# An output projection whose matmuls stand in source order on TensorE, with another pace of attention and eight k tiles left for later

## The chip, the cores and the metric

The kernel runs on one core of a Trainium2 chip. The time is the device time of one execution in microseconds; the figure shown is the median of three executions. The engines are named as in the profile: PE (TensorE, matmuls and transposes), DVE (VectorE), ACT (ScalarE), POOL (GpSimd) and SP (SyncE, which only issues transfers).

## The reference

One block of a hybrid network on a sequence of 512 tokens, width D = 2048, all in float32. In short:

```python
u   = rmsnorm(x)                                  # [512, 2048]
p   = u @ w_in                                    # z, conv input, dt, q, six k/v, gates
ys  = ssd_mixer(z, xbc, dt)                       # state space half, 1024 wide
ya  = nsa_mixer(q, kc, vc, ks, vs, kw, vw, gate)  # attention half, 1024 wide
h   = x + concat(ys, ya) @ w_out                  # output projection, 2048 -> 2048
t   = rmsnorm(h)
out = h + (silu(t @ w_gate) * (t @ w_up)) @ w_down   # FFN, 5632 wide
```

The attention half has 4 groups of 4 heads. Each head attends over compressed blocks, over selected blocks and in a window; with 512 tokens the last two are two full causal attentions, here called branches.

## The kernel before

**Products.** Every operand is split in a rounded part (hi, made by `a_hi` on ACT, L124) and the rest (lo, made by a subtraction on DVE, L127). A product of one 128-deep k tile is three matmuls, hi·hi, hi·lo and lo·hi (L233 to L235), 128x512 each. This is the unit in which work is counted: a *k tile*.

**Units.** `run_unit` computes one block of 128 output columns from its k tiles. 41 units of 16 k tiles make p from w_in. Then come 16 units, c0 to c15, of the output projection: their right side is what the state space half (k tiles 0 to 7) and attention (8 to 15) produced. Since the last heads' outputs aren't ready in time, unit c takes only its first NS[c] k tiles (11, 11, then 12); the remainder is made later by *oa steps* (first matmul at L1175 to L1177), which load the rest of w_out anew, add it to what the unit left in DRAM (h1_d) and prepare the FFN's input. Weights arrive by SP (`wraw`), four k tiles at a time, and are split on ACT (`whi`) and DVE (`wlo`) ahead of use.

**What runs between k tiles.** Attention, the evacuations and the state space half are generators. `Sched.tick()` is called once after each k tile and moves each generator on; what a generator yields is the number of ticks until it goes on. Attention of one group makes 32 scores (head, branch, block of 128 queries), in 36 loop steps. A step does: one score (two matmuls, L833 and L834, then a fused maximum on DVE, L837, and the exponential on ACT, L839); a yield of 1; the transposes of the score three steps earlier (LAG, L862), whose result is split to `pth` on ACT and `ptl` on DVE; the normalisation; and a yield of `PACE[...]`, which is 1. After each fourth score the products with v follow (L872, L873, L878, into ps_v). I call four such steps a round. After a pair of heads the output `at` is split to `u`, the right side of the later units. The 128 scores of all groups are counted through as score steps here.

**The evacuation of an output unit** (`ev_os`, L981 to L992): ACT copies PSUM to a tile h1 (L987); POOL issues a transfer that adds x to it (L988), and after four ticks one that stores it to h1_d (L990). While attention's pool is open h1 is one single buffer. Before c15, `pre_last` waits until attention has been issued to its end, then closes attention's pool and opens those of the oa steps and the FFN (Z, A, R, E), which lie on the same memory, and loads h1 of the first four blocks from ACT's queue (L1220; the fourth goes to `rrow`).

**Order.** What the ticks fix is the source order. Around the change a scheduler of the Tile framework makes each engine's order from it: it follows the source's order as a priority but by its own estimate of times lets an instruction that it takes for ready go ahead of one that it takes for late. Most of the FFN's steps are already under `tc.manual_schedule()`, which keeps the source order. Each engine runs its own list strictly in that order.

Of the kernel before, what the change touches and what calls it, by code (L numbers as in the profile page):

```python
# [24 lines left out]
          (0, 6), (2, 3), (6, 5), (7, 6), (5, 6), (3, 6), (4, 6), (1, 6)]  # L25
GRING = 7

NS = [11, 11] + [12] * 14
KSUB = 4
PACE = [1]  # L30
LAG = 3
EB = 5
LEAD = 3
# [36 lines left out]
NU = 41  # L70
# [44 lines left out]
def body(ctx, tc, xT, w_in, w_out, w_gate, w_up, w_down, w1k, w1v, cols, rows, kst, out):  # L115
# [100 lines left out]
    def run_unit(u):  # L216
        if u.pre:
            u.pre()
        if u.need:
            sch.run_until(*u.need)  # L220
        n_u = st["unit"] = st.get("unit", 0) + 1
        if n_u > 6:
            sch.run_until(("evac", n_u - 2))
        p = ps_t() if n_u <= 2 else ps_s() if n_u <= 4 else ps_g()
        p = p[:, 0:u.cols[1] - u.cols[0]]
        for i, k0, n in u.sub:
            issue_split(i)
            for j in range(n):
                if j == 0:
                    issue_split(i + LEAD)  # L230
                k = k0 + j
                ah, al = [t[:, u.cols[0]:u.cols[1]] for t in u.rhs(k)]
                pe.matmul(p, hi_t[i][:, j, :], ah, start=(k == 0), stop=False)  # L233
                pe.matmul(p, hi_t[i][:, j, :], al, start=False, stop=False)  # L234
                pe.matmul(p, lo_t[i][:, j, :], ah, start=False, stop=(k == u.nk - 1))  # L235
                sch.tick()
            del hi_t[i], lo_t[i]

        def evac():
            yield from u.evac(p)  # L240
            sch.flags.add(("evac", n_u))
        sch.add(evac())
# [339 lines left out]
    P2 = {}  # L582
# [203 lines left out]
    def attention():  # L786
# [6 lines left out]
        for g in range(4):  # L793
# [105 lines left out]
            n = len(items)  # L899
            for s in range(n + LAG + 1):  # L900
                if s < n:
                    score(*items[s])
                    if items[s][1:] == (1, 3):
                        sch.flags.add(("h", g, items[s][0]))
                yield 1
                if 0 <= s - LAG < n:
                    trans(*items[s - LAG])
                if s < n:
                    norm(*items[s])
                yield PACE[s % len(PACE)]  # L910
                if 0 <= s - LAG - 1 < n and items[s - LAG - 1][2] == 3:
                    pvmm(*items[s - LAG - 1][:2])
            sch.flags.add(("a", g))
# [42 lines left out]


    def pre_out():
        sch.run_until(*[("gy", t) for t in range(8)])
        P2["ms"] = [(U[:, 0, k], U[:, 1, k]) for k in range(8)]  # L960
        P2["ma"] = [(U[:, 0, 8 + k], U[:, 1, 8 + k]) for k in range(8)]
        for k in range(8):
            h_, l_ = P2["ms"][k]
            t = wp.tile([128, 512], F32, tag="raw", name="gy", bufs=4)
            nc.sync.dma_start(t, gy_d[k])
            mul(pool, t, t, P2["row2"])
            a_hi(h_, t, scale=col(C_SN + k))
            dve.scalar_tensor_tensor(l_, t, col(C_SN + k), f(h_), op0=ALU.mult, op1=ALU.subtract)  # L968
        sch.add(ma_in(P2["at"] + 1))
# [768 lines left out]
    def run_rest():  # L1738
        pre_steps()
        for s in steps[:KD]:  # L1740
            run_step(s)
        with tc.manual_schedule():
            for s in steps[KD:]:
                run_step(s)
            sch.drain()
        for n in ("ta", "E", "ws"):
            close_pool(n)
        right.close()
# [52 lines left out]
    for n, u in enumerate(units):  # L1801
        if n == 4:
            nc.sync.dma_start(kcs(K_AM, NK - K_AM), kst[:, K_AM:NK])
            nc.sync.dma_start(colc[:, C_PE:C_W2], cols[:, C_PE:C_W2])
        run_unit(u)
    run_rest()


# [86 lines left out]
```

## Time and profile before

| | |
|---|---|
| median of three executions | 2248.61 us (2246.32 to 2249.75) |
| the profiled execution | 2251.17 us, span 2249.4 us |
| mean granted clock of PE | 0.988 |
| PE busy | 2164.1 us, 96% of the span |
| DVE / ACT / POOL busy | 1785.6 / 1192.9 / 430.5 us |
| c0 begins, attention ends, first matmul of the oa steps | about 600, 821 and 828 us |

How to read it: a row of windows gives, for a stretch of the span, each engine's busy time with its count of instructions, then the clock that PE was granted (1.00 is full), the busy share of the DMA engines and what they moved. A row of a timeline gives start, duration, engine, line, operation and tiles, and in brackets how long the engine stood idle before it and what ended that. An engine with a q behind its name is its queue, issuing transfers.

### The profile page before, as it was taken

How to read it: one execution, taken by the hardware profiler on the slowest of the kernel's cores; microseconds unless marked ns; L12 is line 12 of the kernel's file. 1: busy time of each engine (PE TensorE's matmuls, PEld its weight loads, DVE VectorE, ACT ScalarE, POOL GpSimd, SP SyncE). 2: the span in 40 equal slices, each digit the busy share in tenths (PEclk: the TensorE clock that was granted, in tenths of full speed). 3: DMA queues.
4: the chain of work that ended last, by engine and by line, in shares of the span. 5: the costliest groups of instructions: out<-in, count | busy, mean ns of one | idle time of the engine just before them, and what ended most of it. 6: DMA issues, size and time to landing. Idle time of an engine off the chain costs nothing. (4 is left out here: it accounts for less than half of the span.)

```text
span 2249.4 us, 35036 instructions
## 1 busy us (share of the span) xinstructions
PE 2164.1 (96%) x12892; PEld 1903.7 (85%) x12892; DVE 1785.6 (79%) x2822; ACT 1192.9 (53%) x1992; POOL 430.5 (19%) x440
## 2 busy tenths in 40 slices
PE   7999999999999988999999999999999899999996
PEld 5888888888877866788888888888888899999996
DVE  7799766678776648888888788888888888988897
ACT  4564456567665646555555555555555443433353
POOL 2011224133241116100000000001000121222222
PEclk9999999999999989999999999999999999999999
DMA  5222343222244447787888878888887969696985
GB/s 178 90 71 76 120 151 101 74 82 74 94 119 121 109 132 213 203 244 210 246 229 241 227 221 240 219 252 229 222 242 221 338 224 318 187 303 167 297 192 143
DMA packets 170860, 417.18 MB, mean 185 GB/s; under 512 B 16848, under 2 KB 24032, under 8 KB 170688
## 3 DMA queue, kind: packets, MB, share of 16 engines
q1 hardware_dynamic: 99200, 246.99, 33.2%
q0 software_dynamic: 28192, 80.91, 18.5%
q10 hardware_dynamic: 43296, 87.04, 10.7%
q8 instruction: 101, 1.65, 0.3%
q14 instruction: 71, 0.58, 0.1%
HBM read 353.80 MB, written 57.41 MB: 183 GB/s over the span
## 5 line engine op out<-in xcount | busy, mean ns | idle before, releaser
L124 ACT ACTIVATE R<-Z 128x1024 fp32r<-128x1024 f32 (+4 forms) x461 | 417.2, 918 | 450.2 <-DVE Z L136 308.1
L127 DVE TENSOR_TENSOR R<-Z,R 128x1024 fp32r<-128x1024 f32 (+4 forms) x371 | 388.8, 1057 | 27.7 <-ACT R L124 22.6
L234 PE MATMUL ps_g<-u,whi 128*128 128x512 f32 x782 | 309.2, 395 | 2.1 <-DVE u L968 2.1
L233 PE MATMUL ps_g<-u,whi 128*128 128x512 f32 x782 | 310.2, 398 | 0.0
L235 PE MATMUL ps_g<-u,wlo 128*128 128x512 f32 x782 | 309.4, 396 | 0.0
L1171 PE MATMUL ps_s<-u,R 128*128 128x512 f32 (+1 forms) x1136 | 252.9, 350 | 8.6 <-ACT A L1381 8.4
L127 DVE TENSOR_TENSOR wlo<-wraw,whi 128x512 fp32r<-128x512 f32 x212 | 161.2, 762 | 80.7 <-ACT whi L124 80.1
L1171 PEld LDWEIGHTS ps_s<-u,R 128*128 128x128 f32 x1136 | 184.6, 188 | 40.9 <-ACT A L1381 15.1
L124 ACT ACTIVATE whi<-wraw 128x512 fp32r<-128x512 f32 x212 | 132.5, 625 | 138.3 <-PE ps_g L234 95.8
L234 PEld LDWEIGHTS ps_g<-u,whi 128*128 128x128 f32 x782 | 147.5, 189 | 31.3 <-DVE u L968 3.3
L235 PEld LDWEIGHTS ps_g<-u,wlo 128*128 128x128 f32 x782 | 147.4, 189 | 28.8
L233 PEld LDWEIGHTS ps_g<-u,whi 128*128 128x128 f32 x782 | 147.2, 189 | 27.4
L1171 PE MATMUL ps_t<-u,R 128*128 128x512 f32 (+1 forms) x608 | 131.8, 347 | 0.3 <-DVE R L127 0.3
L1171 PE MATMUL ps_g<-u,R 128*128 128x512 f32 (+1 forms) x608 | 131.8, 347 | 0.3 <-DVE R L127 0.3
L1171 PE MATMUL ps_g<-T,R 128*128 128x512 f32 (+1 forms) x568 | 128.1, 353 | 3.6 <-DVE R L127 3.6
L1171 PE MATMUL ps_s<-V,R 128*128 128x512 f32 (+1 forms) x560 | 124.6, 350 | 5.0 <-ACT V L124 3.3
L1171 PE MATMUL ps_s<-T,R 128*128 128x512 f32 (+1 forms) x584 | 126.3, 347 | 0.7 <-DVE R L127 0.7
L127 DVE TENSOR_TENSOR E<-Z,R 128x1024 fp32r<-128x1024 f32 (+1 forms) x90 | 109.2, 1213 | 3.1 <-ACT R L124 1.8
L1171 PEld LDWEIGHTS ps_t<-u,R 128*128 128x128 f32 x608 | 98.9, 188 | 14.8 <-DVE R L127 0.7
L1171 PEld LDWEIGHTS ps_g<-u,R 128*128 128x128 f32 x608 | 98.9, 188 | 14.8 <-DVE R L127 0.7
L136 DVE TENSOR_TENSOR A<-ps_g,A 128x512 f32<-128x512 f32 (+1 forms) x110 | 71.1, 653 | 48.5 <-PE ps_g L1171 39.1
L1171 PEld LDWEIGHTS ps_g<-T,R 128*128 128x128 f32 x568 | 94.6, 192 | 17.5 <-DVE R L127 4.0
(490 smaller groups left out, 5544.6 us busy)
## 6 DMA issues: line engine op xcount, KB each, us to landing
Z<-in_w_up SPq DMA_DIRECT2D x95, 512.0 KB, 5.2
Z<-in_w_gate SPq DMA_DIRECT2D x94, 512.0 KB, 6.8
wraw<-in_w_in SPq DMA_DIRECT2D x164, 256.0 KB, 2.6
g_d<-A ACTq DMA_DIRECT2D x22, 1792.0 KB, 15.0
Z<-in_w_gate POOLq DMA_DIRECT2D x39, 512.0 KB, 7.0
Z<-in_w_up POOLq DMA_DIRECT2D x38, 512.0 KB, 8.7
Z<-in_w_down SPq DMA_DIRECT2D x56, 320.0 KB, 5.2
Z<-in_w_down SPq DMA_DIRECT2D x40, 384.0 KB, 4.1
```

What stands on the lines that cost most here:

```text
L124: act.activation(dst, src, AF.Copy, scale=scale)
L127: eng.tensor_tensor(dst, src, f(hi), ALU.subtract)
L136: eng.tensor_tensor(o, a, b, ALU.add)
L233: pe.matmul(p, hi_t[i][:, j, :], ah, start=(k == 0), stop=False)
L234: pe.matmul(p, hi_t[i][:, j, :], al, start=False, stop=False)
L235: pe.matmul(p, lo_t[i][:, j, :], ah, start=False, stop=(k == u.nk - 1))
L1171: pe.matmul(o, w, x, start=start, stop=(k == n - 1 and o is q), skip_group_check=not fresh[0])
```

## The change

Four edits. NS of the last unit goes from 12 to 8, so that its oa step makes 8 k tiles instead of 4. PACE goes from 1 to 2, 2, 2, 3 in turn, for as long as w_in's units run; from `pre_out` (ahead of c0) on attention takes PACE_OUT, 1, 2, 1, 2. And all output units are issued under a manual schedule for PE alone: its instructions stand in source order from c0 on, while ACT, DVE, POOL and SP are still ordered by the scheduler.

```diff
-NS = [11, 11] + [12] * 14
+NS = [11, 11] + [12] * 13 + [8]
 KSUB = 4
-PACE = [1]
+PACE = [2,2,2,3]
+PACE_OUT = [1,2,1,2]
...
                 if s < n:
                     norm(*items[s])
-                yield PACE[s % len(PACE)]
+                yield P2.get("pace", PACE)[s % len(PACE)]
...
     def pre_out():
+        P2["pace"] = PACE_OUT
         sch.run_until(*[("gy", t) for t in range(8)])
...
+        if n == NU:
+            break
         run_unit(u)
+    with tc.manual_schedule(engines={mybir.EngineType.PE}):
+        for u in units[NU:]:
+            run_unit(u)
     run_rest()
```

NU is the number of w_in's units. The number of instructions on PE is the same, 12876; the first 1750 rows of its order and the last 3706 stand as before. Score step 72 stands at k tile 656 of the program before and at 658 now. From score step 68 to 84 there are 122 instructions of DVE and 36 k tiles before, and 124 and 28 now. Lines of the changed kernel are one higher than before behind PACE, and two higher behind `pre_out`.

Three places show what moved. The first is PE where c0 and c1 meet. Before (ps_g_6967 is c0, ps_g_7107 is c1), the two blocks' k tiles alternate, and scores and transposes stand between them:

```order
L235 MATMUL ps_g_7107<-u_91,wlo_7032 128x512
L833 MATMUL ps_s_6392<-kh_5379,rq_5857 128x128
L834 MATMUL ps_s_6392<-kl_5380,rq_5857 128x128
L233 MATMUL ps_g_6967<-u_91,whi_6824 128x512
L233 MATMUL ps_g_7107<-u_91,whi_7031 128x512
L872 MATMUL ps_v_6381<-cph_5930,vpad_3170 128x512
```

Now (c1 is ps_g_6738) a run of scores and transposes without any k tile stands behind c0, and c1 begins after it:

```order
L879 MATMUL ps_v_6522<-ptl_6440,v_4947 128x128
L834 MATMUL ps_s_6680<-kh_5097,rq_5293 128x128
L835 MATMUL ps_s_6680<-kl_5098,rq_5293 128x128
L863 MATMUL ps_t_6687<-ident_74,e_6581 128x128 x2
L834 MATMUL ps_s_6694<-kh_5097,rq_5293 128x256
L835 MATMUL ps_s_6694<-kl_5098,rq_5293 128x256
L863 MATMUL ps_t_6701<-ident_74,e_6617 128x128 x3
L834 MATMUL ps_s_6710<-kh_5097,rq_5293 128x384
L835 MATMUL ps_s_6710<-kl_5098,rq_5293 128x384
L863 MATMUL ps_t_6717<-ident_74,e_6646 128x128 x4
L834 MATMUL ps_s_6726<-kh_5097,rq_5293 128x512
L835 MATMUL ps_s_6726<-kl_5098,rq_5293 128x512
L234 MATMUL ps_g_6738<-u_91,whi_6507 128x512
```

The eleven k tiles of c0 no longer share their stretch with those of c1.

The second is ACT behind the evacuation of c3, where the load of c3's h1 (to rrow_75) stands; it waits for c3's store. Before:

```order
L987 ACTIVATE h1_7559<-ps_g_7389 128x512
L124 ACTIVATE e_6636<-e_6636,em_6637 128x128
L124 ACTIVATE e_6657<-e_6657,em_6658 128x256
L124 ACTIVATE whi_7615<-wraw_7455 128x512
L124 ACTIVATE pth_6605<-ps_t_6643 128x2x128
L1220 DMA rrow_75<-h1_d_66 128x512
L124 ACTIVATE pth_6605<-ps_t_6664 128x3x128
L839 ACTIVATE e_6699,em_6700<-e_6699,em_6700 128x384
```

Now:

```order
L989 ACTIVATE h1_7172<-ps_g_7026 128x512
L840 ACTIVATE e_7168,em_7169<-e_7168,em_7169 128x256
L125 ACTIVATE pth_7112<-ps_t_7185 128x3x128
L125 ACTIVATE whi_7219<-wraw_7074 128x512
L840 ACTIVATE e_7202,em_7203<-e_7202,em_7203 128x384
L125 ACTIVATE pth_7112<-ps_t_7209 128x4x128
L125 ACTIVATE pth_7238<-ps_t_7240 128x128
L840 ACTIVATE e_7231,em_7232<-e_7231,em_7232 128x512
L1222 DMA rrow_75<-h1_d_66 128x512
L125 ACTIVATE whi_7263<-wraw_7125 128x512
```

The load stood four instructions behind the evacuation and stands seven behind it now; those ahead of it follow scores and transposes of two steps more.

The third is the end of attention. On PE before, the last transposes and products with v stand right ahead of the first matmul of the oa steps (ps_g_8599):

```order
L878 MATMUL ps_v_7984<-ptl_7974,v_6237 128x384
L878 MATMUL ps_v_7984<-pth_7973,v_6237 128x256
L878 MATMUL ps_v_7984<-ptl_7974,v_6237 128x256
L878 MATMUL ps_v_7984<-pth_7973,v_6237 128x128
L878 MATMUL ps_v_7984<-ptl_7974,v_6237 128x128
L1175 MATMUL ps_g_8599<-u_91,R_8524 128x512
L1176 MATMUL ps_g_8599<-u_91,R_8524 128x512
```

Now the last products stand inside c13 (ps_g_8378), with 4 k tiles of it, 12 of c14 and 8 of c15 behind them:

```order
L879 MATMUL ps_v_8353<-ptl_8334,v_6134 128x256
L879 MATMUL ps_v_8353<-pth_8333,v_6134 128x128
L879 MATMUL ps_v_8353<-ptl_8334,v_6134 128x128
L234 MATMUL ps_g_8378<-u_91,whi_8341 128x512
L235 MATMUL ps_g_8378<-u_91,whi_8341 128x512
L236 MATMUL ps_g_8378<-u_91,wlo_8342 128x512
```

The first matmul of the oa steps (ps_g_8582) stands behind c15 (ps_g_8537):

```order
L234 MATMUL ps_g_8537<-u_91,whi_8479 128x512
L235 MATMUL ps_g_8537<-u_91,whi_8479 128x512
L236 MATMUL ps_g_8537<-u_91,wlo_8480 128x512
L1177 MATMUL ps_g_8582<-u_91,R_8518 128x512
L1178 MATMUL ps_g_8582<-u_91,R_8518 128x512
```

So 24 k tiles now separate attention's last product from it, where there was none.

On ACT at the same place, before, with the last split of attention's transposes (pth), its last result (u_91<-at), the three loads of h1 and the first split of the oa steps' weights (R_8524<-Z_8523):

```order
L124 ACTIVATE pth_7973<-ps_t_8015 128x3x128
L124 ACTIVATE pth_7973<-ps_t_8027 128x4x128
L886 ACTIVATE fo_8061<-ps_v_7984 64x512
L124 ACTIVATE u_91<-at_7879 128x512
L1220 DMA A_8522<-h1_d_66 128x512 x3
L124 ACTIVATE R_8524<-Z_8523 128x640
L987 ACTIVATE A_8522<-ps_g_8543 128x512
```

Now two evacuations (h1_8458 of c13 and h1_8507 of c14) stand between attention's last result and the loads of h1:

```order
L887 ACTIVATE fo_8437<-ps_v_8353 64x512
L125 ACTIVATE u_91<-at_8236 128x512
L125 ACTIVATE whi_8462<-wraw_8383 128x512
L989 ACTIVATE h1_8458<-ps_g_8378 128x512
L125 ACTIVATE whi_8479<-wraw_8415 128x512
L989 ACTIVATE h1_8507<-ps_g_8461 128x512
L1222 DMA A_8516<-h1_d_66 128x512 x3
L125 ACTIVATE R_8518<-Z_8517 128x640
L989 ACTIVATE A_8516<-ps_g_8537 128x512
```

The evacuation of c14 was ahead of the end of attention, and is now behind it, right ahead of the loads and of the weights' first split.

## The prediction

> **What bounds the kernel now.** I read the page's totals and slices first, then the windows around the change, then PE's waits there, and last the queues behind those waits.
>
> ```profile
> span 2249.4 us, 35036 instructions
> PE 2164.1 (96%) x12892; PEld 1903.7 (85%) x12892; DVE 1785.6 (79%) x2822; ACT 1192.9 (53%) x1992; POOL 430.5 (19%) x440
> PE   7999999999999988999999999999999899999996
> PEclk9999999999999989999999999999999999999999
> ```
>
> PE works 2164.1 of 2249.4 us, so the whole kernel has 85 us of idle PE, and the change adds and removes no matmul. It can win only idle PE and half-clock time, or make more of it. Windows (PE, PEld, DVE, ACT, POOL busy; clock; DMA share; GB/s) say where that lies:
>
> ```profile
> 400.00:600.00 200.00, 200.00 (x1071) 171.76 (x1070) 152.21 (x410) 130.17 (x308) 61.17 (x68) 1.00 0.23 75
> 601.60:654.80 53.20, 47.24 (x258) 38.60 (x258) 47.23 (x122) 39.14 (x92) 24.32 (x21) 1.00 0.39 121
> 620.00:640.00 20.00, 15.93 (x90) 12.73 (x89) 19.58 (x49) 16.47 (x38) 13.04 (x10) 1.00 0.28 90
> 680.00:700.00 20.00, 17.13 (x79) 14.17 (x78) 10.12 (x32) 10.98 (x29) 2.77 (x4) 0.91 0.47 132
> 690.00:692.00 2.00, 2.00 (x6) 1.53 (x6) 1.05 (x3) 2.00 (x5) 0.00 (x0) 0.50 0.24 80
> 700.00:720.00 20.00, 20.00 (x105) 17.07 (x104) 12.70 (x39) 12.91 (x31) 5.00 (x6) 1.00 0.47 119
> 800.00:820.00 20.00, 18.48 (x94) 15.17 (x94) 7.20 (x18) 5.95 (x14) 1.43 (x3) 0.99 0.15 41
> 820.00:832.00 12.00, 5.07 (x15) 4.02 (x14) 3.73 (x5) 4.59 (x8) 0.86 (x1) 0.50 0.61 209
> 832.00:834.00 2.00, 2.00 (x7) 1.55 (x6) 0.42 (x1) 0.72 (x2) 0.00 (x0) 0.68 1.01 328
> 880.00:900.00 20.00, 14.35 (x69) 11.39 (x68) 15.33 (x18) 12.78 (x20) 7.92 (x11) 0.83 0.40 126
> ```
>
> While w_in's last units run PE is full (400 to 600). Three holes follow: the output projection's first two blocks (from 601.6, where DVE is 98% busy at 620 to 640), one stall at 688, and the end of attention at 820, where PE also falls to half clock. Between them PE is full again. PE's own rows name the waits:
>
> ```profile
> 621.55 0.50 PE L234 MATMUL ps_g<-u,whi 128*128 128x512 f32 x1 [1.06 <-DVE u L968]
> 634.74 0.33 PE L833 MATMUL ps_s<-kh,rq 128*128 128x128 f32 x1 [1.20 <-DVE em L837]
> 637.31 0.47 PE L872 MATMUL ps_v<-cph,vpad 128*128 128x512 f32 x1 [1.61 <-DVE at L136]
> 688.53 0.30 PE L862 MATMUL ps_t<-ident,e 128*128 128x128 f32 x1 [2.87 <-DVE ptl L127]
> 689.13 0.39 PE L235 MATMUL ps_g<-u,wlo 128*128 128x512 f32 x1
> 689.36 0.40 PE L233 MATMUL ps_g<-u,whi 128*128 128x512 f32 x1
> 817.41 0.66 PE L862 MATMUL ps_t<-ident,e 128*128 128x128 f32 x4 [0.60 <-DVE ptl L127]
> 818.75 0.49 PE L878 MATMUL ps_v<-pth,v 128*128 128x512 f32 x1 [0.69 <-ACT pth L124]
> 828.49 0.79 PE L1175 MATMUL ps_g<-u,R 128*128 128x512 f32 x1 [6.93 <-ACT R L124]
> ```
>
> **The change, part by part.** A 512-wide matmul follows the last by 0.23 us (689.13, 689.36), so one k tile of three is 0.68 us: my unit of cover.
>
> *Pace of attention under w_in: nothing.* The order has score step 72 at k tile 656 before and 658 now; attention waits for each group's q, k and v, so the new pace spreads the rounds but does not move the end. PE was full from 400 to 600, so there is no gain; a loss is bounded by the worst hole a few rounds make, 2 us. I take 0.
>
> *First two blocks: a loss.* From score step 68 to 84 (601.60 to 654.80) PE had 47.24 us of work and DVE 122 instructions in 47.23 us. The order now puts 124 DVE instructions there and 28 k tiles where 36 stood: 41.8 us of PE work. The eight k tiles run later, so the stretch breaks even at 53.2 - 5.4 = 47.8 us. DVE alone needs 124 x 0.387 = 48.0 us if it never waits, 54.0 with the 6.0 us that it idled before. PE also has the unfilled run of scores and transposes ahead of block c1. That is 0 to +6; the three waits above show PE already waiting for DVE where it had more cover, and the multiplications by the norm on POOL now share their stretch with more of attention's rotary work. I take +4, with ends 0 and +10.
>
> *The stall at 688: goes.* Its cause stands on ACT and POOL:
>
> ```profile
> 678.71 0.92 POOL L988 DMA_DIRECT2D h<-in_xT  x1 [6.92 <-ACT h L987]
> 684.54 0.58 POOL L990 DMA_DIRECT2D h_d<-h  x1 [4.92 <-DMA h<-in_xT]
> 680.86 0.36 ACT L124 ACTIVATE pth<-ps_t 128x256 fp32r<-128x256 f32 x1
> 686.90 0.36 ACTq L1220 DMA_DIRECT2D rrow<-h_d  x1
> 687.30 0.49 ACT L124 ACTIVATE pth<-ps_t 128x384 fp32r<-128x384 f32 x1 [6.08 <-DMA h_d<-h]
> ```
>
> The scheduler hoisted the load of block c3's h1 (rrow) into ACT's queue, where it holds everything behind it until c3's store lands, 8.2 us after its accumulation was issued (678.71 to 686.90). Four instructions stood between c3's evacuation and the load, so ACT stood 6.08 us and PE 2.87, then ran at half clock (the 690 to 692 row; the 0.91 of 680 to 700 makes it some 3.5 us, 1.7 lost): 4.6 in all. The load is still on ACT now, but seven instructions behind the evacuation, and what they wait for takes PE three scores, two rows of transposes and five k tiles: by the spacing above 4.9 us, plus 2 for DVE and ACT. ACT should stand about 2 us (0.7 for the evacuation + 8.2 - 6.9), until 8.9, and the next transposes that need it stand three more k tiles and ten products further, after 9.6 us. So -4.6; the ends are -4.6 and 0, if PE in strict order meets the wait anyway.
>
> *End of attention: smaller, not gone.* Before, nothing was left for PE:
>
> ```profile
> 822.95 0.63 ACT L124 ACTIVATE u<-at 128x512 fp32r<-128x512 f32 x1 [0.76 <-DVE at L136]
> 822.97 5.62 SPq L1110 DMA_DIRECT2D Z<-in_w_out  x7
> 827.70 0.74 ACT L124 ACTIVATE R<-Z 128x640 fp32r<-128x640 f32 x1 [4.12 <-DMA Z<-in_w_out]
> 807.30 0.87 POOL L988 DMA_DIRECT2D h<-in_xT  x1 [7.30 <-ACT h L987]
> 811.50 0.56 POOL L990 DMA_DIRECT2D h_d<-h  x1 [3.32 <-DMA h<-in_xT]
> h<-in_xT POOLq DMA_DIRECT2D x11, 256.0 KB, 4.6
> A<-in_xT POOLq DMA_DIRECT2D x1, 256.0 KB, 8.0
> ```
>
> It cost 1.5 (800 to 820), 6.93, and about 3.3 of half clock (1.0 around 820, 2.4 from 828.49 to 833.3): 11.8. Now 24 k tiles (4 of c13, 12 of c14, 8 of c15) follow attention, 16 us, and the loads of w_out start under them. But a store chain takes the loads' place. The first a_hi of the new weights waits for c14's store of h1, whose tile lies where the weights' pools open; c14's evacuation waits for c13's store, as both use one buffer. Evacuation to landed store is 0.9 + 4.2 + 2.4 = 7.5 us (807.30, 811.50, and 684.54 to 686.90). c13's accumulation now runs beside seven loads, as the one that took 8.0 instead of 4.6 did: landed 10.9 us after c13's last k tile, where c14's evacuation wants it at 8.2 (12 k tiles). So that evacuation is 2.7 late, and the first matmul of the new weights comes 2.7 + 7.5 + 0.8 (the a_hi) = 11.0 after c14's end, where c15's eight k tiles cover 5.4: a hole of 5.6, with 2.4 of half clock again. 8.0 against 11.8 is -3.8. Without the collision the hole is 2.9. By the row at 688, where 2.87 us idle was followed by clock 0.50, that still costs 1.7, so -7.2; the other end is 0. [...]
>
> *Eight k tiles behind attention: about -1.* The block's remainder is 8 k tiles instead of 4, so 2.7 us of PE work moves into the stretch before the FFN, where PE has 5.65 us idle (880 to 900):
>
> ```profile
> 879.23 1.06 ACT L124 ACTIVATE R<-Z 128x1024 fp32r<-128x1024 f32 x1 [3.91 <-DMA Z<-in_w_gate]
> ```
>
> It fills at most 2.7 of a wait for that DMA, and brings its own loads to the same queues. I take -1, ends -2.7 and +1.
>
> **Sum:** +4 - 4.6 - 3.8 - 1 = -5.4 on the profiled execution's 2251.17 us (1.8 of it around the span), which makes 2245.8. That execution is 2.56 above the median of the runs, 2248.61, so 2243.2 there, as are the times below.
>
> **Rivals.**
> *R1, well covered:* DVE keeps up in the first two blocks (+1) and the accumulation isn't slowed by the loads (-7.2). For it: 680 to 800 shows DVE far from full. Against: 620 to 640 at 98%, and the 8.0 row. +1 - 4.6 - 7.2 - 1 = -11.8: 2236.8.
> *R2, strict order, slower:* PE follows the source, so it waits at a transpose or at ps_v whenever DVE or ACT is late, where the scheduler had put k tiles ahead. Eleven rounds of four steps stand between step 84 and the end. The last round of before, without cover, waited 0.60 at its transposes and 0.69 at its products (817, 818), 1.3 in all; with two or three k tiles a step I take 0. At 1.0 it is +11: -5.4 + 11 = +5.6, 2254.2. It decides from (5.4 + 4.5) / 11 = 0.9 a round. For it: the new pace puts only one or two k tiles between a score and its transposes. Against: DVE is busy 12.70 of 20 us at 700 to 720, so it is seldom late.
> *R3, it doesn't do what it says:* the hole behind attention stays as long, set by the stores instead of the loads (0 for -3.8). +4 - 4.6 - 1 = -1.6: 2247.0. For it: the chain above is only 3.8 shorter than what it replaces, and one more slow transfer eats that.
>
> **How the numbers follow.** A measurement of this kernel tells about 0.2%, 4.5 us, from no change: bounds 2244.1 and 2253.1. The forecast gets 0.36, and its own range is 2238 to 2249: one term at its other end at a time. R1 0.26, R2 0.22, R3 0.16. The time is the forecast's, 2243.2. To hold 8 in 10 the range reaches from 2234 (R1 with the gap before the FFN filled, 2.7) to 2254.5 (R2). Faster: R1 and a little over half of the forecast, 0.46. Same: the rest of it and most of R3, 0.30. Slower: R2 and the tail of R3, 0.24.
>
> **What would show it.** In the windows after: from c0 to the middle of c1 DVE over 90% and PE idle 6 to 10 us; the load of rrow on ACT still waiting, about 2 us, with no half clock near it; between the last matmul of c15 and the first of L1177 a hole of 5 to 6 us put down to ACT, with the accumulation of c13 near 8 us; from c1 to c13 PE full. Waits on pth, ptl or em spread over those blocks would make R2 right; an accumulation of 4 to 5 us and a hole of 3, R1; a hole of 7 or more, R3. New holes under w_in, which I cost at nothing, would make the prediction wrong in a way that no rival covers.

## The result and the profile after

The changed kernel takes 2261.4 us (median of 4 runs, 2258.62 to 2262.93), the kernel before 2247.57 beside it (2246.32 to 2249.75). The ratio is 1.0059, 95% interval 1.0042 to 1.0077: 13.8 us slower, where 2243.2 was forecast and the range ended at 2254.5. The page of the profiled execution (2260.72 us), its totals and slices:

```profile
span 2259.0 us, 34978 instructions
PE 2173.3 (96%) x12892; PEld 1908.9 (85%) x12892; DVE 1799.4 (80%) x2821; ACT 1196.9 (53%) x1991; POOL 435.3 (19%) x439
PE   7999999999989989999999999999999899999996
PEclk8999999999979999999999999999999999999999
```

The page hides the loss: PE's share is the 96% of before, and of the clock's digits only that of slice 12 (from 621 us on) shows it, with a 7 where a 9 stood (the 8 of slice 1 at the start costs under 0.4 us up to PE's 1200th matmul). PE is busy 9.2 us longer with the same matmuls, which is what half clock looks like in a total. The windows of the changed kernel (columns as in the prediction) show where:

```profile
600.00:620.00 20.00, 17.25 (x88) 13.83 (x86) 15.57 (x38) 13.29 (x33) 9.14 (x11) 0.91 0.40 120
620.00:640.00 20.00, 16.75 (x61) 13.80 (x60) 19.57 (x31) 9.25 (x19) 14.93 (x10) 0.58 0.28 78
640.00:660.00 20.00, 16.63 (x66) 12.89 (x67) 15.11 (x42) 13.76 (x33) 4.24 (x4) 0.74 0.37 96
680.00:700.00 20.00, 20.00 (x108) 16.94 (x107) 13.41 (x44) 14.13 (x36) 2.35 (x3) 1.00 0.38 94
700.00:820.00 120.00, 120.00 (x616) 100.61 (x615) 73.75 (x212) 70.79 (x169) 14.31 (x20) 1.00 0.43 116
820.00:840.00 20.00, 12.90 (x50) 10.03 (x50) 2.25 (x3) 4.01 (x7) 2.86 (x4) 0.79 0.59 163
1800.00:1850.00 50.00, 45.80 (x379) 44.78 (x378) 39.43 (x56) 19.58 (x32) 12.49 (x8) 1.00 0.65 221
```

Three things stand here. From 600 to 660 PE idles 9.37 us, and the clock falls short of full speed by 1.8 + 8.4 + 5.2 = 15.4 us; before, these rows had 5.96 us of idle and clock 1.00. At 820 there is still a hole. And from 1800 on, far behind everything that the prediction looked at, PE is short again. The windows of the kernel before that the prediction doesn't show:

```profile
600.00:620.00 20.00, 18.96 (x108) 15.57 (x108) 14.54 (x39) 12.83 (x31) 4.27 (x4) 1.00 0.41 129
640.00:660.00 20.00, 19.15 (x96) 16.04 (x95) 17.00 (x49) 14.72 (x36) 7.87 (x10) 1.00 0.48 136
1800.00:1850.00 50.00, 49.27 (x407) 48.22 (x407) 44.47 (x61) 19.82 (x33) 12.90 (x8) 1.00 0.71 244
```

Half clock is counted here where PE is busy: a 128x512 matmul then follows the last by 0.43 us (838.24 to 838.67 in the changed kernel) instead of 0.23 (602.23 to 602.46). In the changed kernel half clock lasts from 616.4 to 636.9, from 640.3 to 650.5 and again from 831.4 to 841.6; PE is busy 18.46 and 8.47 us of the first two stretches, so about half of that, 13.5 us, is lost there, and 2.6 us of the third:

```profile
616.40:636.90 20.50, 18.46 (x67) 15.50 (x67) 20.24 (x33) 10.33 (x23) 15.68 (x11) 0.50 0.27 77
640.30:650.50 10.20, 8.47 (x21) 6.08 (x22) 7.24 (x16) 5.25 (x12) 2.59 (x2) 0.50 0.37 117
836.37:841.60 5.23, 5.23 (x12) 3.96 (x13) 2.30 (x4) 2.62 (x5) 0.87 (x1) 0.50 0.60 145
```

PE's rows of the changed kernel (timeline) name the waits:

```profile
614.16 0.50 PE L234 MATMUL ps_g<-u,whi 128*128 128x512 f32 x1 [1.54 <-ACT u L125]
640.78 0.79 PE L234 MATMUL ps_g<-u,whi 128*128 128x512 f32 x1 [2.35 <-ACT u L125]
836.37 0.80 PE L1177 MATMUL ps_g<-u,R 128*128 128x512 f32 x1 [7.10 <-ACT R L125]
1815.58 0.38 PE L1179 MATMUL ps_t<-V,R 128*128 128x256 f32 x1 [1.79 <-DVE R L128]
```

To compare stages I take the same instruction of ACT in each trace, counted from the end, and say how much later it stands than in the profiled execution of before. The marks: *first oa*, the first matmul of the oa steps (828.49 before, of PE); *FFN*, 936.70; *down*, 1754.94, ahead of the down projection; *end*, the span, 2249.40.

| kernel | median, us | of before, same chip | ratio, 95% interval | first oa | FFN | down | end |
|---|---|---|---|---|---|---|---|
| the change | 2261.40 | 2247.57 | 1.0059, 1.0042 to 1.0077 | +7.9 | +1.8 | +0.2 | +9.6 |
| e1 | 2257.68 | 2251.63 | 1.0033, 1.0016 to 1.0050 | +6.8 | +1.4 | +2.7 | +8.1 |
| e2 | 2259.53 | 2251.63 | 1.0036, 1.0021 to 1.0051 | +0.2 | +1.4 | +0.8 | +11.0 |
| e3 | 2260.78 | 2251.63 | 1.0043, 1.0029 to 1.0056 | +7.6 | +6.6 | +4.3 | +3.7 |
| e4 | 2260.49 | 2251.63 | 1.0044, 1.0029 to 1.0058 | +4.9 | +0.6 | -3.3 | +7.8 |
| e5 | 2278.91 | 2250.91 | 1.0127, 1.0110 to 1.0144 | +26.3 | +28.2 | +30.4 | +32.6 |
| e6 | 2259.84 | 2250.91 | 1.0044, 1.0028 to 1.0059 | +5.0 | +5.0 | +4.5 | +8.2 |
| e7 | 2255.58 | 2250.91 | 1.0023, 1.0009 to 1.0036 | +1.1 | -4.0 | -2.2 | +6.1 |
| e8 | 2250.58 | 2250.91 | 0.9999, 0.9985 to 1.0013 | +0.2 | -4.7 | -8.8 | -4.8 |
| e9 | 2263.70 | 2249.18 | 1.0055, 1.0036 to 1.0073 | +4.8 | +2.7 | -0.9 | +10.7 |
| e10 | 2264.79 | 2249.18 | 1.0060, 1.0040 to 1.0079 | +6.1 | +5.3 | +0.7 | +9.7 |
| e11 | 2251.87 | 2249.18 | 1.0009, 0.9994 to 1.0024 | +3.6 | -1.7 | -4.5 | +4.7 |
| e12 | 2252.39 | 2250.55 | 1.0004, 0.9993 to 1.0016 | +0.3 | -9.0 | -13.2 | -2.6 |
| e13 | 2259.41 | 2250.55 | 1.0035, 1.0022 to 1.0048 | +8.1 | +3.4 | +4.1 | +9.6 |
| e14 | 2247.92 | 2250.55 | 0.9989, 0.9979 to 0.9999 | +3.9 | -4.6 | -8.4 | -6.7 |
| e15 | 2248.08 | 2251.89 | 0.9981, 0.9968 to 0.9993 | +1.9 | -6.6 | -7.1 | -1.1 |
| e16 | 2254.11 | 2251.89 | 1.0009, 0.9995 to 1.0023 | +4.9 | -1.8 | -1.6 | +7.0 |

The marks come from one profiled execution each, and the runs of one kernel lie up to 18 us apart, so single marks are good to a few us only (the profiled execution is the fastest of its runs in e3 and e12, the slowest in e2 and e5); what rests on less is read from the medians. Kernels with NS = 8 have four k tiles (2.7 us) less in front of the first mark and as much more behind it. The change's own row reads: 7.9 lost up to the first oa step, 6.1 won by the FFN, level at the down projection, 9.4 lost in it.

### The profile page after: what moved, and what is told of

Its sections match the earlier page's. It is cut to its first block, busy times and chain, and to the rows that moved or that the text cites. A ratio compares the mean times of both kernels' runs of the same rounds, so it can differ in the third digit from the quotient of the medians.

```text
span 2259.0 us, 34978 instructions
## 1 busy us (share of the span) xinstructions
PE 2173.3 (96%) x12892; PEld 1908.9 (85%) x12892; DVE 1799.4 (80%) x2821; ACT 1196.9 (53%) x1991; POOL 435.3 (19%) x439
## 5 line engine op out<-in xcount | busy, mean ns | idle before, releaser
L234 PE MATMUL ps_g<-u,whi 128*128 128x512 f32 x778 | 317.5, 408 | 3.9 <-ACT u L125 3.9
L235 PE MATMUL ps_g<-u,whi 128*128 128x512 f32 x778 | 308.3, 396 | 2.7 <-DVE u L970 2.6
L236 PEld LDWEIGHTS ps_g<-u,wlo 128*128 128x128 f32 x778 | 147.2, 189 | 30.4
L1173 PE MATMUL ps_g<-u,R 128*128 128x512 f32 x584 | 131.3, 349 | 0.0
L125 ACT ACTIVATE R<-A 128x1024 fp32r<-128x1024 f32 (+3 forms) x76 | 71.0, 934 | 86.6 <-DVE A L137 61.5
L137 DVE TENSOR_TENSOR Z<-Z 128x1024 f32<-128x1024 f32 (+5 forms) x96 | 104.2, 1085 | 6.9 <-POOL E L137 3.9
```

The source lines that it names most:

```text
L125: act.activation(dst, src, AF.Copy, scale=scale)
L137: eng.tensor_tensor(o, a, b, ALU.add)
L1173: pe.matmul(o, w, x, start=start, stop=(k == n - 1 and o is q), skip_group_check=not fresh[0])
```

## The experiments

The questions, in the order in which they came: which of the change's edits costs; why the down projection, whose instructions the diff doesn't touch, lost 9.4 us; and what the thin stretch from 600 to 660 and the hole behind attention cost by themselves. Lines in the fences are those of each kernel's own source.

**Places of the weight blocks (e1, e2).** The weights of oa steps and FFN arrive in blocks, and for each block `place` seeks a free stretch in the zones Z, A and E by the age of what lay there. The remainder of c15 is now a block of 8 k tiles instead of 4, so it takes another place, and by that most later blocks do: 160 of the 175 of the down projection, by the tables of e1 and e2. A load waits for those who used its place before. e1 gives the changed kernel the places of before in the down projection, e2 gives the kernel before those of the change.

```diff
+RAW_AT = ("236Z24 237Z8 ...").split()   # block: zone and place
+HL_AT = ("324.0R0 324.1R11 ...").split()
...
-            got = place(b)
+            got = put(raw_at.get(str(nxt["raw"])), b.n, lambda: place(b))
```

> The changed kernel with one thing undone: from the down projection's first block on, the weights' blocks and their split copies are put at the places that they had in the kernel before (a table of places instead of the search by age). Theory P (places): by 1770 us the two kernels stand at the same time, and the changed one loses its 9.5 us in the down projection, where its loads got other places and so wait for other blocks; then about 2252 us. Theory S (strict order on PE loses the time in the first two blocks, and it is never regained): no change, about 2261 us.

> The reverse: the kernel before, with the changed kernel's places in the down projection alone. Theory P: about 2257 us (+9.5), with the loss between 1800 and 1930 us of the span. Theory S: about 2248 us.

e2 puts the loss into the kernel before: level until 1755 (+0.8), then 10.2 us later by the end; by the ratio it is 8.1 us up (0.0036 of 2251.63). Its window:

```profile
1800.00:1850.00 50.00, 46.06 (x372) 45.45 (x371) 38.35 (x56) 18.43 (x30) 13.37 (x8) 0.97 0.65 226
```

49.27 of before became 46.06, as in the change (45.80). e1 takes back 5.9 of the 13.8 by the ratios, and loses 5.4 instead of 9.4 behind 1755. So the places cost by themselves; what is left in e1 was lost earlier, or comes with the changed arrival of blocks. Which loads come late by it was not followed in the traces.

**The edits apart (e3 to e8).** e3 is the change without its NS of 8; e4 leaves c0 and c1 to the scheduler; e5 is the kernel before with PE in source order alone, e6 with the paces alone, e7 with the NS alone; e8 is e7 with the places of before. Its expectation speaks of the down projection, but its tables begin at block 19, where e1's begin at 236: they cover nearly the whole FFN.

```diff
# e3, against the change
-NS = [11, 11] + [12] * 13 + [8]
+NS = [11, 11] + [12] * 14
# e4, against the change
-        if n == NU:
+        if n == NU + 2:
...
-        for u in units[NU:]:
+        for u in units[NU + 2:]:
# e5, against before
+        if n == NU:
+            break
         run_unit(u)
+    with tc.manual_schedule(engines={mybir.EngineType.PE}):
+        for u in units[NU:]:
+            run_unit(u)
# e6, against before
-PACE = [1]
+PACE = [2,2,2,3]
+PACE_OUT = [1,2,1,2]
...
-                yield PACE[s % len(PACE)]
+                yield P2.get("pace", PACE)[s % len(PACE)]
...
+        P2["pace"] = PACE_OUT
# e7 and e8, against before (e8 with tables of places from block 19 on)
-NS = [11, 11] + [12] * 14
+NS = [11, 11] + [12] * 13 + [8]
```

> The changed kernel with the last unit at 12 k tiles again, PE's source order and the paces kept. Theory P: the blocks have their old sizes, so the places are those of before and the loss in the down projection goes; the first blocks' loss is regained at the FFN's start as in the changed kernel: 2250 us, give or take 3. Theory S: 2261 us or a little more.

> The changed kernel, but PE's source order begins at c2 instead of c0, so the scheduler orders the first two units again. The clock should stay at full between 615 and 655 us (it lost 15 us there). Theory P: the first blocks' loss was regained at the FFN's start anyway, and the down projection's loss stays: 2259 us, give or take 3. Theory S: about 2247 us.

> The kernel before with PE's source order for the output units alone; paces and NS as before. By the first runs the change is a sum of two losses: about 8 us until the first matmul of the oa steps (mark W), whose larger part is half clock between 615 and 655 us, and about 8 us in the down projection from places that NS = 8 brings; and of one gain of about 6 us at the FFN's start, also with NS = 8. If source order makes the loss before W: W 7 us later than in the kernel before and +8 us at the end. If the paces make it: no difference.

> The kernel before with the two paces alone; the scheduler orders PE. If the paces make the loss before W (with the first two units left to the scheduler the clock still fell at 620 to 660): W 4 to 7 us later and +4 to +8 us. If source order makes it: no difference, within 2 us.

> The kernel before with the last unit's 8 k tiles alone. By the sum above: W 3 us earlier (4 k tiles moved behind it), the stall near 937 us gone (-6 at the mark 976), and +8 in the down projection: about +2 us in all. If the gain at the FFN's start in the changed kernel was only lost time regained, nothing is gained here and it is +8.

> As the run before, but in the down projection the blocks lie where they lay before (replayed places). If NS = 8 gives 6 us at the FFN's start and only places cost the 8 us: -4 to -6 us, faster than both kernels. If the replayed places don't help as little as in the first run: +2 us.

The paces alone cost 8.9 us (e6), the NS alone 4.7 (e7), together 13.6 of the measured 13.8. Paces and order together cost 9.2 (e3), so the order adds nothing where the paces have changed. By itself it costs 28 (e5). e8 takes the 4.7 of e7 away again: with NS = 8, too, the cost lies in the places, here those of the whole FFN. Its trace wins 4.1 us between the FFN's mark and the down projection's, where e7 loses 1.8, and loses 4.0 instead of 8.3 behind it.

Where the paces lose, e6's windows show; the scheduler still orders PE there:

```profile
600.00:620.00 20.00, 18.01 (x91) 14.59 (x89) 15.68 (x38) 12.58 (x31) 9.25 (x11) 0.91 0.42 116
620.00:640.00 20.00, 15.96 (x84) 13.77 (x82) 19.72 (x43) 13.14 (x33) 10.88 (x9) 0.75 0.17 50
640.00:660.00 20.00, 18.31 (x77) 14.38 (x77) 18.20 (x52) 14.28 (x34) 3.87 (x3) 0.83 0.31 92
680.00:700.00 20.00, 19.59 (x103) 16.54 (x101) 11.79 (x42) 12.97 (x34) 2.88 (x4) 1.00 0.53 145
```

The half clock between 600 and 660 is there without the source order (its shortfall is 1.8 + 5.0 + 3.4 = 10.2 us), and the stall at 688 is gone without it: 19.59 of 20 us at full clock in the last row. Both come with the pace alone. For the stall the pace isn't needed, though: e5, with the order alone, has no such stall around its c3 either (PE idles 0.89 us from 740 to 760, at clock 1.00). Leaving c0 and c1 to the scheduler (e4) brings the first mark 3.0 us forward, and a ratio whose interval overlaps the change's: no cure.

Why the order alone is so dear is read from the programs: with the old pace 22 scores stand in the source between c0 and c1 without a k tile (74 to 96), with the new one four (76 to 80). e5's windows show PE behind DVE through that run:

```profile
620.00:640.00 20.00, 14.11 (x54) 9.02 (x55) 19.31 (x54) 16.62 (x42) 12.70 (x13) 0.76 0.18 55
640.00:660.00 20.00, 14.23 (x55) 11.19 (x55) 17.42 (x51) 13.75 (x36) 7.57 (x7) 0.67 0.21 67
```

e3 and e7 bear on two more places. All traces with an NS of 12 (before, e2, e3, e5, e6) show a wait of 3.5 to 3.8 us at one and the same matmul of the FFN's start; of those with 8 only e10 waits there for over 1 us (1.40). PE's row of before, and two rows of e3:

```profile
936.83 5.06 PE L1171 MATMUL ps_g<-T,R 128*128 128x256 f32 x15 [3.55 <-DVE R L127]
```

```profile
836.03 0.80 PE L1177 MATMUL ps_g<-u,R 128*128 128x512 f32 x1 [5.13 <-ACT R L125]
943.43 5.06 PE L1173 MATMUL ps_g<-T,R 128*128 128x256 f32 x15 [3.76 <-DVE R L128]
```

The other row of e3 is the hole behind attention, 2.0 us shorter than in the change: c15 then covers it with 12 k tiles. Before, half clock surrounded the wait at 936; the change has 1.00 from 936 to 944, and before had:

```profile
936.00:944.00 8.00, 7.17 (x26) 6.23 (x27) 7.93 (x12) 5.07 (x8) 0.61 (x1) 0.59 0.57 133
```

**Is it POOL and DVE that make PE thin at 600 to 660? (e9, e10)** The waits at 614 and 640 are for `u`, made from gy, which POOL multiplies by the norm; POOL also has the rotary embedding of group 3's q there, and DVE the normalisation of the exponentials. e9 leaves out POOL's half of the rotary embedding of the last group's q, which changes the output; e10 moves twelve normalisations, those of three heads, from DVE to ACT.

```diff
# e9
-            rope2(ap, sw, ro)
+            if g < 3:
+                rope2(ap, sw, ro)
# e10
-                if br:
+                if br and (g, h) not in NORM_ACT:     # (2,0), (2,1), (2,2)
```

> The changed kernel; it leaves out POOL's half of the rotary embedding of the last group's two blocks of q (four operations of 1.3 to 1.8 us on POOL between 619 and 637 us). In the changed kernel DVE's normalisations (L849) take 0.35 to 0.55 us where POOL stands still and 1.1 to 3.2 us where POOL works beside them, and PE waits behind them and falls to half clock. Theory L (the new paces put POOL's rotary work of the last group beside the multiplications by the norm, DVE is held up by POOL, PE's thin use halves its clock): the stretch from 612 to 656 us shortens and W comes 4 to 10 us earlier than in the changed kernel. Rival (PE's strict order alone): W moves by less than 2 us.

> The changed kernel with all work, but the normalisations of group 2's first three heads go to ACT in both branches (ACT is 46% busy there), instead of DVE. Theory L: DVE no longer waits for POOL in these (3.2, 1.9, 1.3 us and others), so W comes 3 to 8 us earlier. Rival (not DVE's wait but the number of its instructions, or strict order): within 2 us of the changed kernel.

The first mark comes 3.1 and 1.8 us earlier, the medians stay (1.0055 and 1.0060 against 1.0059). POOL's and DVE's work there is a part of the wait at most; neither removal paid.

**What does the half clock cost? (e11)** Zero matmuls (a zero weight tile, so that the sums don't change) are put among c0's k tiles: ten at the first and three at each of the next seven, 31 in all.

```diff
+FILL = {(0, 0): (8, 2), **{(0, k): (2, 1) for k in range(1, 8)}}
...
+                fill(p, hi_t[i][:, 0:n, :], ahead, k == 0)   # pe.matmul(p, zero, w, ...)
                 pe.matmul(p, hi_t[i][:, j, :], ah, start=(k == 0), stop=False)
+                fill(p, hi_t[i][:, 0:n, :], mid)
```

> The changed kernel with 31 more matmuls in c0 that add zero (weights of zero, 7 us of PE at full clock), ahead of its k tiles where PE waits. They can't make any work ready earlier; they only keep PE busy. If the half clock (15 us lost between 615 and 650) follows from PE's thin use and is a cost of its own: the clock stays at 1.00 or nearly, and W comes 5 to 10 us earlier though there is more work. If PE only waits for DVE and POOL there, and the clock costs nothing: W 0 to 7 us later.

Useless work made the kernel 11 us faster: +2.7 instead of +13.8 against before. Its windows:

```profile
600.00:620.00 20.00, 18.75 (x106) 15.83 (x105) 15.46 (x39) 14.44 (x34) 9.87 (x12) 1.00 0.42 122
620.00:640.00 20.00, 15.76 (x73) 12.44 (x72) 19.10 (x36) 10.96 (x24) 15.39 (x11) 0.83 0.29 90
640.00:660.00 20.00, 18.30 (x97) 14.78 (x98) 16.95 (x51) 13.73 (x36) 2.84 (x3) 1.00 0.34 96
820.00:840.00 20.00, 12.85 (x45) 9.85 (x44) 3.63 (x5) 5.40 (x10) 3.36 (x5) 0.74 0.65 196
```

DVE is as full as it was, but the clock's shortfall fell from 15.4 to 3.4 us. That reads as if the half clock were a cost of its own, but four things speak against taking the 11 us as its price. The trace accounts for 4.9 us of them (end +4.7 against +9.6); the profiled execution was 4 us above the median of its runs (2255.92, 2251.87), and what the others saved beyond it no trace shows. The edit isn't zero matmuls alone: the scheduler, which still orders DVE, ACT and POOL, gave all three another order between 614 and 645 us. Other kernels lost less to the clock and gained little: e4 and e9 have 13.7 and 17.1 us of half clock there instead of 30.7, at ratios of 1.0044 and 1.0055. And e1, whose instructions up to the down projection are those of the change, shows that a better clock is in part paid back in waits:

```profile
600.00:620.00 20.00, 17.38 (x86) 13.79 (x84) 15.46 (x38) 12.85 (x32) 8.60 (x10) 0.88 0.40 110
620.00:640.00 20.00, 14.86 (x61) 11.85 (x61) 19.77 (x28) 9.76 (x21) 14.61 (x10) 0.69 0.26 79
640.00:660.00 20.00, 16.76 (x80) 12.74 (x80) 17.88 (x52) 14.03 (x35) 4.52 (x4) 0.91 0.39 106
```

Its shortfall is 10.4 us instead of 15.4 and its idle 11.0 instead of 9.37; the first mark stands 1.1 us earlier, not 5. So with e11's zero matmuls the clock did rise (0.91, 0.58 and 0.74 in the three rows became 1.00, 0.83 and 1.00); how much of the loss is the clock's by itself stays open.

**What does the hole behind attention cost? (e12)** The h1 of c13 and c14 gets buffers of the weights' pool, four deep, instead of the single one in attention's pool (c15 is evacuated when that pool is closed).

```diff
-            if "att" in pools:
+            if "att" in pools and c >= 13:
+                t = wp.tile([128, 512], F32, tag="raw", name="h1", bufs=4)
+            elif "att" in pools:
```

> The changed kernel, but from c13 on the tile h1 lies among the weights' raw buffers (which stay open) instead of in attention's pool, and no longer in one single buffer. If the hole of 7.1 us behind attention is set by the stores of c13 and c14 (the store chain of the prediction): the hole shrinks to under 2 us, its half clock goes, and W comes 7 to 10 us earlier. If it is set by the loads of w_out (5 to 7 us from issue to landing, issued at the end of attention, under 16 us of k tiles) or by something else: W unchanged. At the end of the kernel the gain stays, unless the FFN's start takes it back.

The hole is gone; the window of e12 there:

```profile
820.00:840.00 20.00, 20.00 (x88) 16.34 (x87) 5.53 (x10) 7.77 (x14) 6.71 (x11) 1.00 0.91 268
```

The first oa step comes 7.6 us earlier than in the change, the end 12.2, and the median falls by 12 us (ratio 1.0059 to 1.0004). So it was the stores of h1, one behind the other through one buffer, that held the hole open, as the prediction's chain said, and taking the chain away is worth 12 us. The edit undoes both of its links at once, the one shared buffer and its place on the memory where the next pools open; which of them would do was not tried.

**Together (e13 to e16).** e13 is e11 with the places of e1 and 24 idle matmuls behind c15. e14 has 54 zero matmuls in c0 and c1, h1 elsewhere and the places of before; e15 the last two; e16 the first two.

```diff
# e13, beside e11 and the places
+                    pe.matmul(q, hi_t[i][:, j, :], ah, start=True, stop=True)   # 24 times
# e14 and e16
+FILL = {(0, 0): (8, 4), (0, 1): (3, 3), (0, 2): (2, 1), (0, 3): (2, 8), (0, 4): (2, 2), (0, 5): (2, 4), (0, 6): (2, 1),
+        (0, 7): (2, 1), (1, 0): (5, 0)}
# e15
+FILL = {}
```

> The changed kernel with three things: the 31 matmuls of zero in c0 (they gained about 10 us in the median of the run before), 24 idle matmuls behind c15 (5.5 us of the hole of 7.1; nothing reads them), and the places of before in the down projection. If the half clock is a cost of its own and the places cost 8 us: 2 to 8 us below the kernel before. If a gain before W is taken back at the FFN's start: at the kernel before, within 2 us.

> The changed kernel with all three remedies: matmuls of zero where PE waits in c0 and c1 (54 of them), h1 of c13 and c14 among the raw buffers, and the places of before in the down projection. The changed kernel stood 13.3 us above the kernel before; -10 for the clock, -7 to -10 for the hole, -5 to -8 for the places: 10 us below the kernel before, give or take 4. If the FFN's start takes the gain back (its loads set the pace): no more than 3 us below.

> The changed kernel with the h1 of c13 and later in buffers of the weights' pool and with the weight blocks of the down projection at the places of the kernel before; no added matmuls. Theory A, the places act by themselves: until 1755 us as e12 (13.2 ahead of the kernel before), and behind it a loss of 1.7 to 5.5 us instead of the 8.3 to 11.6 of all kernels with the places of after; span 8 to 11 us under the 2249.4 of before, median 4 to 8 us under e12's, so 2 to 6 us under the kernel before. Theory B, the places help only beside the added matmuls: a loss of 9 to 11 behind 1755, the median as e12's (1.8 above before).

> The changed kernel with the h1 of c13 and later elsewhere and the 54 added zero matmuls in c0 and c1, the weights' places left as they are. If the two gains add up (12.0 and 11.1 us of the median): 9 us under the kernel before, first matmul of the oa steps some 4 us before that of the kernel before. If the added matmuls cost there what they save, as e14 seems to say: that matmul 3 to 5 us after that of the kernel before, 8 to 9 us ahead at 1755, a loss of 9 to 11 behind it, and the median 1 to 6 us above the kernel before.

e15 has the lowest ratio, 0.9981 (0.9968 to 0.9993), 4.3 us under before by the ratio, and e14 with 0.9989 just clears 1. Set beside each other, the ratios tell the factors apart as far as the pairs go:

| factor | pairs, change of the ratio |
|---|---|
| places of before, down projection | change to e1 -0.0026; e12 to e15 -0.0023; e16 to e14 -0.0020 |
| places of before, nearly the whole FFN | e7 to e8 -0.0024 |
| h1 elsewhere | change to e12 -0.0055; e1 to e15 -0.0052 |
| zero matmuls | 31: change to e11 -0.0050; 54: e12 to e16 +0.0005, e15 to e14 +0.0008; 31 and 24 idle ones: e1 to e13 +0.0002 |
| h1 elsewhere, and 54 zero matmuls for 31 | e11 to e16 0.0000 |

The places of the down projection are worth 0.0020 to 0.0026, 4.5 to 5.9 us, in each of three pairs, whatever else is in the kernel. A single pair is hardly larger than its uncertainty (about 0.002); that all agree, and e2 with them, carries the reading. Behind 1755 the eight traces with NS = 8 and its own places, and e2, lose 8.3 to 11.6 us; four with the places of before (e1, e8, e13, e14) lose 1.7 to 5.5, and e15, against its expectation, 6.1. The three with NS = 12 and their own places (e3, e5, e6) lie between a gain of 0.6 and a loss of 3.7. The medians, not these marks, carry the verdict. One window of e15 against the change's 45.80:

```profile
1800.00:1850.00 50.00, 48.83 (x405) 48.02 (x405) 43.31 (x60) 18.60 (x32) 15.39 (x9) 1.00 0.68 230
```

The zero matmuls' gain was not found again: neither 54 of them with h1 elsewhere nor 31 in e13 bring anything. The traces say the same ahead of the hole. In the four kernels without zero matmuls whose program is the change's up to there (the change, e1, e12, e15) ACT evacuates c3 at 693.5 to 696.8 us; with the 31 it does so at 691.1 in e11 but at 695.0 in e13, ahead of e13's idle matmuls and with the same order on every engine; with the 54 at 699.8 and 698.8 (e16, e14). So e13's idle matmuls don't explain its loss against e11, and why e11's runs are fast stays open. Whether h1 elsewhere would add to e11's gain was not tested, since e16 has 54 zero matmuls, not 31.

## Why the prediction was wrong

**Under w_in: nothing.** It was so up to 600: PE is busy 199.53 of the 200 us from 400 on. But the prediction took "does not move the end" for "costs nothing". The pace decides which score, which rotary step and which multiplication of gy fall into c0 and c1, and e6 charges 8.9 us for the two paces together; which of them costs was not tried.

**First two blocks: +4, ends 0 to +10. This is the first step that failed.** Idle rose by 3.4 us (5.96 to 9.37), inside the bounds; but the term counted idle alone. Half clock was not in it, though it stood in the term for the end of attention; while PE was busy it took 13.5 us. Together 16.9, over four times the term. What else changed ahead of the first oa step goes against it: the idle from 660 to 680 (-0.8), the stall at 688 with its half clock (-4.6), four k tiles less (-2.7), the waits at 817 and the half clock around 820 (-1.5 and -1.0), and a hole of 7.10 for 6.93 (+0.2). The sum is +6.5, and the mark measured +7.9. That is bookkeeping of one trace: where the time went, not what the clock would cost by itself. That the paces bring this loss is shown by e6; the prediction named DVE's and POOL's crowding as the reason, and e9 and e10 show that to be a part of it at most.

**The stall at 688: -4.6. Right.** 680 to 820 has PE full at clock 1.00. The pace alone does it (e6), and so does the order alone (e5). ACT stands 3.23 us instead of the predicted 2 at the load of rrow, which goes out at 705.07, 8.7 us after c3's accumulation was issued (the row names PE; the load's own wait is not in it), and no one waits for it:

```profile
705.07 0.35 ACTq L1222 DMA_DIRECT2D rrow<-h_d  x1
705.52 0.63 ACT L125 ACTIVATE whi<-wraw 128x512 fp32r<-128x512 f32 x1 [3.23 <-PE ps_t L863]
```

**End of attention: -3.8. The mechanism was right, the size wrong.** The hole is 7.10 instead of 5.6, as long as before, and half clock costs 2.6 instead of 2.4; only the waits at 817 and the half clock around 820 are gone: 9.7 against the 11.8 of before, so -2.1. A hole of 7 or more was the sign of rival R3, and it came true for this place. The chain of the changed kernel, evacuation, accumulation and store of c13 and c14:

```profile
816.95 0.88 POOL L990 DMA_DIRECT2D h<-in_xT  x1 [4.89 <-ACT h L989]
822.85 0.56 POOL L992 DMA_DIRECT2D h_d<-h  x1 [5.03 <-DMA h<-in_xT]
825.58 0.60 ACT L989 ACTIVATE h<-ps_g 128x512 f32<-128x512 f32 x1 [6.69 <-DMA h_d<-h]
826.47 0.87 POOL L990 DMA_DIRECT2D h<-in_xT  x1 [3.07 <-ACT h L989]
832.39 0.56 POOL L992 DMA_DIRECT2D h_d<-h  x1 [5.05 <-DMA h<-in_xT]
835.58 0.74 ACT L125 ACTIVATE R<-Z 128x640 fp32r<-128x640 f32 x1 [9.40 <-DMA h_d<-h]
```

The sum gave c14 the undisturbed 4.2 us from issue to landing and c13 the slow 8.0. Both took 5.9 (816.95 to 822.85, 826.47 to 832.39), and from c14's evacuation to the weights' split it is 10.0 us instead of 7.5. e12 confirms the chain by taking it away.

**Eight k tiles behind attention: -1, ends -2.7 to +1. Missed, on the other side.** The NS brings the FFN's mark 4.0 us forward by itself (e7), and 4.8 in the change against e3. From the first oa step to the FFN the change wins 6.1 us, though 2.7 us more work stands there: the wait of 3.55 with its half clock at 936 is absent. (Over all traces this stretch wins 2.1 to 9.3 us with 8 k tiles, but 0.8 in e10, and at most 1.0 with 12.) Moved work that fills a wait can't bring more than 2.7; that the other places of the blocks removed the wait is my reading, not tested apart.

**The sum lacked a term: the down projection.** This is the second step that failed. I asked what the block of 8 k tiles brings to the queues "before the FFN" and stopped there. Its length changes the places of most later blocks, and that alone costs 4.5 to 5.9 us (three pairs), in e2 8.1. None of the rivals had it.

**R2, strict order.** Its sign came true, its mechanism didn't: from 700 to 820 no wait stands in any round (120.00 of 120 us). With the paces as they are the order costs nothing (e3 against e6), at the old pace 28 us, in one run of 22 scores and not in eleven rounds. **R1** is out: the accumulation took 5.9, the hole stayed.

The sum by what was measured: paces and order +9.2 (e3), NS +4.7 (e7), 13.9 for 13.8, each good to about 3 us.

## What to carry to other kernels

Where PE becomes thin, ask for the clock too: 3.4 us more idle came with 13.5 of lost clock. Don't take that figure for a price: 5.0 us less of it brought 1.1 us in e1, and useless matmuls won 11 us in one kernel and nothing in three others. Where a planner hands out memory by age, a changed block length changes the place of most later loads, so the last stage of the kernel belongs into the prediction of an edit in its middle. And a chain of stores through one buffer ends a stage later than the transfers seem to say: other buffers at its end were worth 12 us here.

## What the runs showed of the hardware

**Half clock after waits of at most 1.54 us.** In the changed kernel the clock falls at about 616.4 after waits of 1.54, 0.37 and 0.41 us, and in e11 after 0.63, 0.61 and 0.66. Windows of 2 us of the change, then of e11:

```profile
616.00:618.00 2.00, 1.39 (x4) 0.69 (x5) 1.94 (x8) 1.03 (x4) 0.88 (x2) 0.60 0.79 226
630.00:632.00 2.00, 2.00 (x11) 2.00 (x11) 1.94 (x4) 0.34 (x2) 2.00 (x2) 0.50 0.01 4
```

```profile
618.00:620.00 2.00, 1.39 (x13) 1.18 (x12) 2.00 (x4) 1.65 (x3) 2.00 (x3) 1.00 0.00 0
622.00:624.00 2.00, 1.62 (x5) 1.32 (x6) 2.00 (x5) 1.54 (x4) 1.22 (x1) 0.73 0.30 51
626.00:628.00 2.00, 2.00 (x19) 2.00 (x18) 1.23 (x6) 1.31 (x5) 1.98 (x2) 0.92 0.05 15
```

In e11 the clock is back after some 3.4 us. In the change it stays at half for 20 us, through rows where PE is busy 2.00 of 2 us; PE has no wait from 624.75 to 635.15. Those rows hold 128x32 matmuls, which e11 ran at 618 to 620 at full clock; whether they, or the short waits between, held the clock down was not isolated. Between 100 and 2200 us half clock comes in stretches of 3.4, 13.7, 6.8, 6.8 and 3.4 us in the trace of before, and of 20.5, 10.2, 10.2 and 3.4 in that of the change; what sets these lengths, and what wait is enough for a fall, no run here shows.

**DVE was slow beside POOL.** The same normalisation of 128x384 takes 0.48 us in one place of the changed kernel and 3.21 in another (from 618.82 on; its row is one of the groups of instructions from 618.1 to 622.1, with busy us and mean ns), where POOL multiplies:

```profile
592.23 0.48 DVE L849 TENSOR_SCALAR e<-e,em,gat 128x384 f32<-128x384 f32 x1
L849 DVE TENSOR_SCALAR e<-e,em,gat 128x384 f32<-128x384 f32 x1 | 3.2, 3209 | 0.0
619.30 1.28 POOL L134 TENSOR_TENSOR ro<-sw,kc 128x512 f32<-128x512 f32 x1
620.53 1.28 POOL L134 TENSOR_TENSOR gy<-gy,row 128x512 f32<-128x512 f32 x1
```

Of the 64 instructions of this line in the changed kernel, the 51 without POOL's arithmetic beside them take 0.33 to 0.55 us, the 13 with it 0.34 to 3.21. So DVE's 19.57 busy us from 620 to 640 (31 instructions, where before 49 stood in 19.58) were in part waiting, by an estimate from these rows: 0.48 and the two multiplications of 1.28 make 3.04 of the 3.21 us, as if DVE had stood still through both. No run isolates that. The prediction's price of 0.387 us for one instruction, an average, was too low just where POOL works. How much of the end it is worth, e9 bounds: no gain in the median.
